# One operand in PSUM for rotary embedding, softmax combination, branch merge and attention division, with an order of steps to match

## The chip, the cores and the metric

The kernel runs on one core of one Trainium2 chip. The metric is the device time of one execution in microseconds (us), taken as the median of several runs; less is better. Engine names in the rows: PE is TensorE (PEld its weight loads), DVE is VectorE, ACT is ScalarE, POOL is GpSimd, SP is the queue that issues most of the DMAs.

## The reference, cut to what matters

The reference is a two-layer generator trunk with 256 latent and 256 context tokens of width 1024. Each layer normalizes and modulates its input, projects it, and runs three branches: latent attention with a rotary key (A), a long convolution (B) and differential attention (C). Then the branches are merged by sigmoid gates and projected, and an MLP follows. The pieces that the change touches:

```python
def apply_rope(x, cos, sin):                      # rotary embedding
    x1, x2 = x[..., :half], x[..., half:]
    return concatenate([x1 * cos - x2 * sin, x2 * cos + x1 * sin], axis=-1)
...
p = softmax(q @ k.T * scale); o = p @ v           # attention; the division comes after p @ v here
...
o = o1 - lam * o2                                 # differential attention: two maps, then a norm
rmsnorm(o, g) * (1.0 - lam_init)
...
m = g_a * (ya @ w_br_a) + g_b * (yb @ w_br_b) + g_c * (yc @ w_br_c)    # merge
y = m @ w_out
```

Layer 0 works on all 512 tokens, layer 1 on the 256 latent ones only (its keys and values still take 512).

## The kernel before, in words

**Matmuls.** Every large product is made of three matmuls: each operand is split into a high part (a cast, `hi`) and the rest (a subtraction, `lo`), and hi·hi, hi·lo and lo·hi are summed in one PSUM bank (`mm3`, L278 to L280). So for each piece of weights (a "unit" of 128x1024) somebody must cast (L230) and somebody subtract (L218), and each activation goes through the same in `split2` (ACT copies, L284, DVE subtracts, L285).

**PSUM.** There are eight banks of 128x512: two each named `s`, `g` and `t`, one `o`, one `mod`. `bank(tag)` hands out the banks of a tag in turn, and the next user of a bank waits until its last reader is done. `bank2` lets some steps of layer 1 take `mod` instead. SBUF scratch comes from a ring of nine 128x512 tiles (`t2k`).

**Steps.** The program is a list of 562 steps, built by `layer`; `ORDER`, a permutation written into the file, says in which order they are emitted. Within that, the framework places the instructions of neighbouring steps among each other on each engine. `CHOICE` is a table that says for a key which engine does a piece of work (`A` ACT, `D` DVE, `P` POOL, `m` the `mod` bank); what isn't in it goes to a default engine. Keys: `hi`/`lo` + number are a unit's cast and subtraction, `rb` + number the second product of a rotary embedding, `kh` a head's key cast, `v` a value copy, `dup` a duplicate row of the differential attention's operands, `tr` the copy of transposed maps, `sq`, `xe`, `mh`, `ml`, `r`, `rl`, `yx` single elementwise operations.

**The pieces that change.** `rope` works in place on a product in PSUM: a shuffle that swaps halves into SBUF (L794), the product with the cosines into SBUF (L795), the product of the shuffled copy with the sines, on DVE or POOL by `CHOICE` (L797), and the sum back to PSUM (L798). It is called 26 times, 13 in each layer. In the differential attention, step `A` computes two maps (matmul L1221, row maximum L807, Exp on ACT L156, the latter into SBUF tiles), a small factor (L1233, L1234) and the combination of both maps (L1238); step `B` transposes the result on PE (L834), step `C` multiplies it with the values, step `N` normalizes. `normalized` (L818 on) divides by the softmax sums, which PE has transposed into a bank `t` (L827, L828). `branch` multiplies three products with three gates (L1332) and adds them up (L1336).

Of the kernel before, what the change touches and what calls it, by code (L numbers as in the profile page):

```python
# [9 lines left out]
F32 = mybir.dt.float32  # L10
F32R = mybir.dt.float32r
AF = mybir.ActivationFunctionType
ALU = mybir.AluOpType
# [110 lines left out]
def backbone_kernel(ctx: ExitStack, tc: tile.TileContext, t, out):  # L124
# [394 lines left out]
    def startup(first_weights):  # L519
        with tc.tile_pool(name="filt", bufs=1, side="right") as fp, tc.tile_pool(name="start", bufs=1) as sp:  # L520
# [234 lines left out]
            SP.dma_start(out=rs, in_=t["rope_sin"])  # L755
# [34 lines left out]
    def rope(ps, rows, scr=True):  # L790

        a, b = t2k(), t2k()
        v = ps[rows, 0:NL]
        DVE.stream_shuffle(out=b[rows, 0:NL], in_=v, mask=SWAP16)  # L794
        DVE.tensor_tensor(out=a[rows, 0:NL], in0=v, in1=rc[rows, :], op=ALU.mult)  # L795
        rope.n = getattr(rope, "n", -1) + 1
        ENG[pick(f"rb{rope.n}", "D")].tensor_tensor(out=b[rows, 0:NL], in0=b[rows, 0:NL], in1=rs[rows, :], op=ALU.mult)  # L797
        DVE.tensor_tensor(out=v, in0=a[rows, 0:NL], in1=b[rows, 0:NL], op=ALU.add)  # L798
# [18 lines left out]
    def normalized(o, sums, nt, key):  # L817

        s, r, rb = t2k(), smp.tile([128, 4, 2], F32, tag="sr", name="sr", bufs=2), t2k()
        nb = nt // 128  # L820
        cp("oe" + key)(s[:, :nt], o[:, :nt])
        DVE.reciprocal(out=r[:, :nb], in_=sums[:, :nb])
        cp("rb" + key)(rb[:, :nt].rearrange("p (j i d) -> p j i d", i=2, d=64),
                       r[:, :nb].unsqueeze(3).to_broadcast([128, nb, 2, 64]))
        pt = bank("t")
        for j in range(nb):
            PE.transpose(pt[:, j * 128:(j + 1) * 128], rb[:, j * 128:(j + 1) * 128], ident)  # L827
        DVE.tensor_tensor(out=s[:, :nt], in0=s[:, :nt], in1=pt[:, :nt], op=ALU.mult)  # L828
        return s
# [327 lines left out]
    def diff(l, nt):  # L1157
# [49 lines left out]
        def A(h, u):  # L1207
            def f():
# [7 lines left out]
                for mi in range(2):  # L1216
# [11 lines left out]
                    p = t2k()  # L1228
# [32 lines left out]
        def N(p):  # L1261
            def f():
                ps = bank("t")
                S["last"] = PE.matmul(ps[:, :nt], lhsT=blk64, rhs=box["sq", p][:, :nt], start=True, stop=True).ins
                r = rstd_of(ps[:, :nt], 64, nt)
                s = t2k()
# [22 lines left out]
    def merge(l, nt, early):  # L1289
# [31 lines left out]
        def branch(n):  # L1321
            def f(u):
                acc = None
                for b, (y, k0, nk, tag) in enumerate((("ya", 0, 4, "s"), ("yb", 4, 2, "s"), ("yc", 6, 2, "g"))):
# [7 lines left out]
                    DVE.tensor_tensor(out=g[:, :nt], in0=g[:, :nt], in1=ps[:, :nt], op=ALU.mult)  # L1332
                    if acc is None:
                        acc = g
                    else:
                        DVE.tensor_tensor(out=acc[:, :nt], in0=acc[:, :nt], in1=g[:, :nt], op=ALU.add)  # L1336
# [341 lines left out]
```

## Time and profile before

| | before |
|---|---|
| median of 3 runs | 1338.29 us (1335.92 to 1344.03) |
| profiled execution, its own time | 1338.25 us |
| its span in the profile | 1336.5 us |
| granted TensorE clock, mean | 0.986 of full speed |
| PE busy | 1286.9 us, 96% |
| DVE busy | 868.0 us, 65% |
| ACT busy | 587.7 us, 44% |
| POOL busy | 278.9 us, 21% |

How to read it: the busy time of an engine is the sum of its instructions' durations without overlaps. PE has 49.6 us of the span in which it does nothing; where it works at a granted clock below 1.00, its instructions take longer. A table of stretches (busy time of each engine and granted clock in each) shows where both lie, and the list of waits says for which instruction of which engine PE waited.

### The profile page before, as it was taken

The page shows a single profiled execution, that of the slowest core. Times are in us where ns is not written, and L with a number is a line of the kernel's source. Part 1 is how long each engine was busy: PE and PEld are TensorE (multiplying, and loading weights), DVE is VectorE, ACT ScalarE, POOL GpSimd, SP SyncE. Part 2 cuts the span into 40 slices and gives each one's busy share as a digit, 9 for nine tenths or more (in the row PEclk, how much of TensorE's full clock was granted, in tenths as well). Part 3 has the DMA queues.
Part 4 walks back from the last instruction along what each step waited for, and adds up shares of the span by engine and source line. Part 5 has one row for each costly group of instructions (what it writes and reads, how often), then busy time and mean ns, then how long its engine had stood idle before and what let it go on. Part 6 is the DMA issues. An engine that isn't in the chain of part 4 may idle for free.

```text
span 1336.5 us, 19918 instructions
## 1 busy us (share of the span) xinstructions
PE 1286.9 (96%) x7934; PEld 1080.9 (81%) x7934; DVE 868.0 (65%) x1406; ACT 587.7 (44%) x1034; POOL 278.9 (21%) x247
## 2 busy tenths in 40 slices
PE   5999999999999999999999999998998999999997
PEld 3566776578888898787787877996887999999997
DVE  4776636955243568886585774587667568876565
ACT  4455543664222334432332332364646655645343
POOL 3212031310002102220100112022234344240210
PEclk8899999999999999999999999998999999999999
DMA  9643243443233324655554553332132455455652
GB/s 278 168 165 106 69 136 99 146 158 95 86 103 95 115 76 141 208 186 174 171 191 141 165 163 119 98 115 68 49 109 79 127 175 176 158 181 181 192 187 95
DMA packets 159791, 185.21 MB, mean 139 GB/s; under 512 B 4880, under 2 KB 149233, under 8 KB 157650
## 3 DMA queue, kind: packets, MB, share of 16 engines
q1 hardware_dynamic: 158162, 182.27, 43.5%
q0 software_dynamic: 928, 1.54, 0.4%
q8 instruction: 62, 1.02, 0.3%
q14 instruction: 31, 0.25, 0.1%
q10 hardware_dynamic: 608, 0.14, 0.0%
HBM read 182.88 MB, written 1.05 MB: 138 GB/s over the span
## 4 chain that ended last, share of the span: by engine, by line
PE 71%; DVE 8%; ACT 2%; DMA 2%; issue 1%; POOL 0%; DVEq 0%; ACTq 0%; SPq 0%; POOLq 0%
PE g L278 13%; PE g L279 13%; PE g L280 13%; PE s L278 8%; PE s L280 8%; PE s L279 8%; DMA raw<-in_w_fc_dram 1%; PE o L847 1%; PE t L834 1%; DVE d L1176 1%; DVE hlo L488 1%; DVE wlo L218 1%; ACT whi L230 1%; DVE t L485 1%; PE mod L346 1%
## 5 line engine op out<-in xcount | busy, mean ns | idle before, releaser
L230 ACT CAST whi<-raw 128x1024 fp32r<-128x1024 f32 x203 | 212.7, 1050 | 442.9 <-PE g L279 206.7
L278 PE MATMUL g<-hhi,whi 128*128 128x512 f32 (+2 forms) x1040 | 355.0, 342 | 5.6 <-ACT ge L1305 1.6
L280 PE MATMUL g<-hhi,wlo 128*128 128x512 f32 (+2 forms) x1040 | 353.0, 340 | 0.5 <-DVE wlo L218 0.5
L279 PE MATMUL g<-hlo,whi 128*128 128x512 f32 (+2 forms) x1040 | 353.0, 340 | 0.2 <-DVE hlo L505 0.2
L218 POOL TENSOR_TENSOR wlo<-raw,whi 128x512 fp32r<-128x512 f32 x144 | 201.9, 1422 | 637.6 <-ACT whi L230 517.2
L218 DVE TENSOR_TENSOR wlo<-raw,whi 128x1024 fp32r<-128x1024 f32 x158 | 197.1, 1249 | 154.1 <-ACT whi L230 147.0
L278 PEld LDWEIGHTS g<-hhi,whi 128*128 128x128 f32 x1040 | 196.1, 189 | 37.5 <-issue 7.0
L279 PEld LDWEIGHTS g<-hlo,whi 128*128 128x128 f32 x1040 | 196.8, 189 | 23.5 <-issue 0.8
L280 PEld LDWEIGHTS g<-hhi,wlo 128*128 128x128 f32 x1040 | 196.9, 189 | 23.2 <-DVE wlo L218 0.9
L382 DVE SCALAR_TENSOR_TENSOR macc<-modr,spad,macc 128x1024 f32<-128x1024 f32 x84 | 111.4, 1356 | 13.0 <-DMA modr<-in_w_mod_dram 12.2
L1358 DVE SCALAR_TENSOR_TENSOR x<-s,modT,x 128x256 f32<-128x256 f32 x95 | 43.4, 479 | 74.5 <-PE s L280 74.3
L280 PE MATMUL s<-hid0h,wlo 128*128 128x512 f32 (+1 forms) x256 | 87.0, 340 | 0.0
L279 PE MATMUL s<-hid0l,whi 128*128 128x512 f32 (+1 forms) x256 | 86.7, 339 | 0.0
L278 PE MATMUL s<-hid0h,whi 128*128 128x512 f32 (+1 forms) x256 | 86.6, 338 | 0.0
L280 PE MATMUL s<-hid1h,wlo 128*128 128x256 f32 (+1 forms) x224 | 72.7, 325 | 0.0
L278 PE MATMUL s<-hid1h,whi 128*128 128x256 f32 (+1 forms) x224 | 72.6, 324 | 0.0
L279 PE MATMUL s<-hid1l,whi 128*128 128x256 f32 (+1 forms) x224 | 72.2, 323 | 0.0
L156 ACT ACTIVATE t<-s,sm 128x512 f32<-128x512 f32 (+1 forms) x91 | 55.4, 612 | 36.9 <-DVE sm L807 36.2
L807 DVE TENSOR_REDUCE sm<-s 128x1 f32<-128x512 f32 (+1 forms) x75 | 51.3, 687 | 25.3 <-PE s L280 20.0
L278 PEld LDWEIGHTS s<-hid0h,whi 128*128 128x128 f32 x256 | 48.4, 189 | 7.3 <-ACT whi L230 0.8
L279 PEld LDWEIGHTS s<-hid0l,whi 128*128 128x128 f32 x256 | 48.0, 187 | 5.9
L280 PEld LDWEIGHTS s<-hid0h,wlo 128*128 128x128 f32 x256 | 48.1, 188 | 5.7
(465 smaller groups left out, 2411.1 us busy)
## 6 DMA issues: line engine op xcount, KB each, us to landing
raw<-in_w_fc_dram SPq DMA_DIRECT2D x64, 1024.0 KB, 5.4
raw<-in_w_in_dram SPq DMA_DIRECT2D x34, 1024.0 KB, 5.3
modr<-in_w_mod_dram SPq DMA_DIRECT2D x48, 512.0 KB, 4.1
raw<-in_w_mod_dram SPq DMA_DIRECT2D x16, 1024.0 KB, 5.0
mq<-in_w_mod_dram SPq DMA_DIRECT2D x16, 512.0 KB, 7.5
raw<-in_w_out_dram SPq DMA_DIRECT2D x8, 1024.0 KB, 5.3
raw<-in_w_in_dram SPq DMA_DIRECT2D x8, 512.0 KB, 3.9
raw<-in_w_br_a_dram SPq DMA_DIRECT2D x8, 512.0 KB, 3.6
```

Of the source, the lines that this page charges most:

```text
L156: ins = ACT.activation(out=out, in_=in_, func=func, **kw).ins
L218: e.tensor_tensor(out=u.lo[:, a:a + w], in0=src[:, a:a + w], in1=u.hi[:, a:a + w].bitcast(F32), op=ALU.subtract)
L230: cp(f"hi{u.id}")(u.hi, src)
L278: PE.matmul(ps, lhsT=ah, rhs=bh, start=first and i == 0, stop=False)
L279: PE.matmul(ps, lhsT=ah, rhs=bl, start=False, stop=False)
L280: PE.matmul(ps, lhsT=al, rhs=bh, start=False, stop=last and i == n - 1)
L346: PE.matmul(box["ps"][32 * j:32 * j + 32, :], lhsT=spad[:, kt, :], rhs=raw[:, 512 * j:512 * (j + 1)], start=kt == 0, stop=kt == KT - 1)
L382: DVE.scalar_tensor_tensor(out=a, in0=raw, scalar=sv, in1=a, op0=ALU.mult, op1=ALU.add)
L485: DVE.scalar_tensor_tensor(out=tt, in0=x[:, kt, c], scalar=amul[l][:, w, kt, s:s + 1], in1=r, op0=ALU.mult, op1=ALU.mult)
L488: DVE.scalar_tensor_tensor(out=hb["lo"][:, kt, c], in0=tt, scalar=sh, in1=hb["hi"][:, kt, c].bitcast(F32), op0=ALU.add, op1=ALU.subtract)
L807: DVE.tensor_reduce(out=sm[:, c0:c0 + nseg], in_=ps.rearrange("p (s k) -> p s k", s=nseg), axis=AX.X, op=ALU.max, negate=True)
L1358: DVE.scalar_tensor_tensor(out=x[:, n, c], in0=ps[:, c], scalar=modT[l][:, goff + n, s:s + 1], in1=x[:, n, c], op0=ALU.mult, op1=ALU.add)
```

## The change

`rope` now multiplies the product in PSUM by the sines first, into SBUF, then by the cosines in place, shuffles the sine product within SBUF, and adds it to PSUM; all four are on DVE, and the keys `rb` are gone. The table of sines is shuffled once at the start so that the result is the same: it is loaded to a new tile `rst`, and a shuffle writes `rs`. `normalized` writes its result to the PSUM bank of the sums when branch A calls it. In the differential attention the second map stays in its PSUM bank (Exp writes in place), and the combination reads it from there; in step `N` the reciprocal root and the scaled result are written to the PSUM bank of the sum of squares. In `branch` the second and third gated products are written back to the PSUM banks of the products, and the last sum is written there too, from where `split2` reads it. `ORDER` has some 25 steps moved by one to three places, and two moved further in layer 1 (step 425, an inverse transform of the convolution branch, and step 450, the normalization of the first pair of heads); the moved steps of the layer 0 MLP are parts of the second layer's modulation, which issue their DMAs from SP. `CHOICE` gains 22 entries and loses 19, 13 of them `rb`.

```diff
-            SP.dma_start(out=rs, in_=t["rope_sin"])
+            rst = fp.tile([128, NL], F32, name="rst")
+            SP.dma_start(out=rst, in_=t["rope_sin"])
+            DVE.stream_shuffle(out=rs, in_=rst, mask=SWAP16)
...
-        DVE.stream_shuffle(out=b[rows, 0:NL], in_=v, mask=SWAP16)
-        DVE.tensor_tensor(out=a[rows, 0:NL], in0=v, in1=rc[rows, :], op=ALU.mult)
-        rope.n = getattr(rope, "n", -1) + 1
-        ENG[pick(f"rb{rope.n}", "D")].tensor_tensor(out=b[rows, 0:NL], in0=b[rows, 0:NL], in1=rs[rows, :], op=ALU.mult)
-        DVE.tensor_tensor(out=v, in0=a[rows, 0:NL], in1=b[rows, 0:NL], op=ALU.add)
+        DVE.tensor_tensor(out=a[rows, 0:NL], in0=v, in1=rs[rows, :], op=ALU.mult)
+        DVE.tensor_tensor(out=v, in0=v, in1=rc[rows, :], op=ALU.mult)
+        DVE.stream_shuffle(out=b[rows, 0:NL], in_=a[rows, 0:NL], mask=SWAP16)
+        DVE.tensor_tensor(out=v, in0=v, in1=b[rows, 0:NL], op=ALU.add)
...
-        DVE.tensor_tensor(out=s[:, :nt], in0=s[:, :nt], in1=pt[:, :nt], op=ALU.mult)
-        return s
+        to = pt if key[0] == "m" else s
+        DVE.tensor_tensor(out=to[:, :nt], in0=s[:, :nt], in1=pt[:, :nt], op=ALU.mult)
+        return to
...
-                    p = t2k()
+                    p = ps if mi else t2k()
...
-                r = rstd_of(ps[:, :nt], 64, nt)
-                s = t2k()
+                r = rstd_of(ps[:, :nt], 64, nt, ps[:, :nt])
+                s = ps
...
-                    DVE.tensor_tensor(out=g[:, :nt], in0=g[:, :nt], in1=ps[:, :nt], op=ALU.mult)
+                    to = g if acc is None else ps
+                    DVE.tensor_tensor(out=to[:, :nt], in0=g[:, :nt], in1=ps[:, :nt], op=ALU.mult)
                     if acc is None:
                         acc = g
                     else:
-                        DVE.tensor_tensor(out=acc[:, :nt], in0=acc[:, :nt], in1=g[:, :nt], op=ALU.add)
+                        to = ps if b == 2 else acc
+                        DVE.tensor_tensor(out=to[:, :nt], in0=acc[:, :nt], in1=ps[:, :nt], op=ALU.add)
+                        acc = to
```

`CHOICE`, the entries that matter near the waits of the rows: new are `hi132`, `hi139`, `lo130`, `lo140`, `lo150`, `v1.3`, `dup1.0.0.1` on DVE and `hi129`, `hi133`, `hi141`, `hi148` on POOL; gone are `kh1.0` from DVE (so ACT does it), `v0.3` from DVE and the `rb` from POOL; two `m` entries (`bktd1.0.0`, `bktm1.3.0`) are gone. `ORDER`, an excerpt of layer 1's differential attention:

```diff
-    (409, 425), (426, 434), 436, (434, 436), 437, 440, 438, 441, 439, (442, 444), 425, (444, 447), 448, 447, 449,
-    453, (450, 453), (454, 461), ...
+    (409, 425), (426, 434), 436, 439, 434, 437, 440, 435, 438, (441, 447), 448, 447, 449,
+    453, (451, 453), 450, 425, (454, 461), ...
```

## Rows read from the trace of the kernel before

**Rows 1.** The page: span, and busy time of each engine.

```profile
span 1336.5 us, 19918 instructions
PE 1286.9 (96%) x7934; PEld 1080.9 (81%) x7934; DVE 868.0 (65%) x1406; ACT 587.7 (44%) x1034; POOL 278.9 (21%) x247
```

**Rows 2.** Forty equal stretches: length, busy time (instructions), granted clock, DMA share, GB/s.

```profile
233.80:267.20 33.40, 30.24 (x163) 19.17 (x162) 30.12 (x58) 21.47 (x54) 12.63 (x13) 1.00 0.41 147
...
367.40:400.80 33.40, 33.40 (x145) 27.01 (x144) 14.36 (x18) 9.52 (x12) 3.25 (x2) 1.00 0.34 105
...
901.80:935.20 33.40, 27.49 (x160) 22.78 (x161) 24.93 (x53) 15.90 (x29) 8.26 (x10) 0.85 0.24 72
...
1002.00:1035.40 33.40, 28.87 (x201) 26.17 (x201) 24.49 (x48) 20.76 (x43) 13.94 (x14) 0.95 0.27 78
```

**Rows 3.** Waits of PE over the span: for whom, us in total, times, longest.

```profile
PE t L834 <- DVE t L1238: 4.8, 5, 1.9
...
PE g L278 <- DVE x L1076: 2.4, 1, 2.4
```

**Rows 4.** DVE in order of time, layer 1: start, duration, what [idle before].

```profile
1006.08 0.45 DVE L794 STREAM_SHUFFLE t<-g 128x256 f32<-128x256 f32 x1
...
1008.62 1.50 DVE L798 TENSOR_TENSOR g<-t 128x256 f32<-128x256 f32 x1 [1.19 <-POOL t L797]
...
1013.19 0.75 DVE L1238 SCALAR_TENSOR_TENSOR t<-t,sm 128x512 f32<-128x512 f32 x1
```

**Rows 5.** POOL in order of time, the same place.

```profile
1007.85 0.74 POOL L797 TENSOR_TENSOR t<-t,rs 128x256 f32<-128x256 f32 x1
1008.54 1.29 POOL L218 TENSOR_TENSOR wlo<-raw,whi 128x512 fp32r<-128x512 f32 x1
```

**Rows 6.** PE in order of time, the same place.

```profile
1013.99 0.66 PE L834 MATMUL t<-ident,t 128*128 128x128 f32 x4 [1.90 <-DVE t L1238]
1015.70 0.38 PE L278 MATMUL g<-hhi,whi 128*128 128x256 f32 x1 [1.05 <-DVE d L1176]
```

**Rows 7.** Two stretches of 4 us there, columns as in rows 2.

```profile
1012.00:1016.00 4.00, 1.05 (x7) 0.72 (x7) 3.74 (x11) 2.91 (x7) 0.95 (x2) 1.00 0.01 2
1016.00:1020.00 4.00, 4.00 (x23) 4.00 (x22) 3.82 (x8) 2.00 (x5) 0.00 (x0) 0.57 0.11 12
```

**Rows 8.** DVE in order of time, layer 0.

```profile
233.89 1.32 DVE L1234 SCALAR_TENSOR_TENSOR sm<-ss,nlam,sm 128x1 f32<-128x1 f32 x1
...
235.74 1.26 DVE L1238 SCALAR_TENSOR_TENSOR t<-t,sm 128x512 f32<-128x512 f32 x1
...
239.30 1.73 DVE L1238 SCALAR_TENSOR_TENSOR t<-t,sm 128x512 f32<-128x512 f32 x1
```

**Rows 9.** PE in order of time, layer 0, the wait behind the last of these.

```profile
241.08 0.33 PE L834 MATMUL t<-ident,t 128*128 128x128 f32 x1 [1.49 <-DVE t L1238]
```

**Rows 10.** Groups by line and shape: busy us, mean ns of one | idle before.

```profile
L458 DVE TENSOR_TENSOR o<-o,t 128x256 f32<-128x256 f32 x26 | 11.1, 427 | 4.2 <-ACT t L454 4.0
...
L1336 DVE TENSOR_TENSOR t<-t 128x512 f32<-128x512 f32 x12 | 8.3, 692 | 0.4
L1332 DVE TENSOR_TENSOR t<-t,s 128x512 f32<-128x512 f32 x12 | 8.2, 684 | 5.7 <-PE s L280 5.7
...
L797 POOL TENSOR_TENSOR t<-t,rs 32x256 f32<-32x256 f32 x9 | 6.8, 759 | 32.2 <-DVE t L794 24.7 <-issue 4.6 <-ACT kh L977 2.9
L797 DVE TENSOR_TENSOR t<-t,rs 32x256 f32<-32x256 f32 x9 | 3.7, 409 | 0.1
```

**Rows 11.** ACT writing to SBUF and to PSUM, by line and shape.

```profile
L454 ACT ACTIVATE t<-x 128x512 f32<-128x512 f32 x2 | 1.3, 631 | 0.5 <-DVE x L1358 0.5
...
L448 ACT ACTIVATE o<-x 128x512 f32<-128x512 f32 x2 | 1.2, 603 | 0.9 <-DVE x L1358 0.8
```

**Rows 12.** DVE in order of time: layer 0's first normalization, from L429 on.

```profile
276.12 0.69 DVE L429 TENSOR_SCALAR t<-t 128x512 f32<-128x512 f32 x1 [2.17 <-PE t L1264]
...
283.39 0.68 DVE L285 TENSOR_TENSOR ycl<-t,ych 128x512 fp32r<-128x512 f32 x1
```

73 rows, old and new, of tables (CHOICE, ORDER) are left out of this document.

## The prediction, as it was put on record

> **What bounds the kernel now.** I read the page's busy times first. PE is busy for 1286.9 of 1336.5 us, DVE for 868.0 [rows 1], so PE sets the time, and a change that touches no matmul can only win back the 49.6 us in which PE does nothing and the stretches in which its granted clock is low. Second, the forty equal stretches: through the layer 0 merge and MLP, from 267 to 868 us, PE misses under 1 us in all, and the stretch 367.40:400.80 stands for those [rows 2]. Whatever the change does there, to the merge of layer 0 and the moved modulation steps, is hidden. Two things are left that it can reach: the layer 0 differential attention (233.80:267.20, PE 30.24 of 33.40, so 3.16 us idle) and two stretches of layer 1 (901.80:935.20, idle 5.91 at a clock of 0.85; 1002.00:1035.40, idle 4.53 at 0.95) [rows 2]. In 15% and 5% of their 33.4 us the low clock costs another 5.0 and 1.7 us at most. That makes 20.3 us, the most that can be won where the change acts; the start and the final norm it hardly touches. Third, the list of waits: the largest one in these places is PE's transposes waiting for the combination of the two maps, 4.8 us in 5 times [rows 3].
>
> **Why those waits are long.** Reader, look at layer 1 around 1007 us. DVE shuffles at 1006.08 [rows 4]; POOL's sine product starts only at 1007.85, and right behind it, at 1008.54, POOL starts a subtraction of 1.29 us [rows 5]. DVE had waited 1.19 us for the product, and its sum (two operands in SBUF) then takes 1.50 us and ends 0.29 us after that POOL subtraction [rows 4, 5], where the same kind of sum with an operand in PSUM takes 0.43 (256 elements, x26) [rows 10]. So a DVE instruction with two SBUF operands waited for POOL's. Everything on DVE behind it is late, up to the combination at 1013.19 [rows 4], and PE stands still for 1.90 us and then 1.05 us [rows 6]. After that its clock falls: 0.57 in 1016 to 1020, following 1.05 us of work in the 4 us before [rows 7]. In layer 0 two combinations take 1.26 and 1.73 us [rows 8] instead of the 0.75 of the one in layer 1 [rows 4], and PE waits 1.49 us behind the second [rows 9].
>
> **Rotary embedding.** Before, 4 operations, in 13 of the 26 calls 3 on DVE and one on POOL; after, 4 on DVE. The costs: product from PSUM 0.41 [rows 10] (the DVE form of L797, which differs only in its source), product in place in PSUM 0.43 (L458) [rows 10], shuffle 0.45 [rows 4], sum 0.43. The shuffle now reads SBUF, which the trace doesn't show; between 0.41 (a product) and 0.45 (the shuffle from PSUM) I take 0.45. DVE gains 13 x 0.41 = 5.3 us of work, POOL loses 13 x 0.76 = 9.9 us [rows 10]. On PE's path this lies at one place for certain, the call of rows 4: DVE's idle 1.19 and the excess of 1.50 over 0.43, 1.07, go; one more product of 0.41 comes: 1.19 + 1.07 - 0.41 = **1.85 us off**, of 2.95 us of PE's waits there. I count it whole, since ACT's and DVE's steps between the sum and the combination all follow that sum. What remains of PE's wait is 1.1 us; a wait of 1.49 us in layer 0 [rows 9] lies in a stretch whose clock stays at 1.00 [rows 2], so I expect no fall here: 4.00 x 0.43 = **1.7 us off** [rows 7], bounds 0 and 1.7.
>
> **Combination from PSUM.** It loses its waits for POOL: in layer 0, 1.26 and 1.73 become 0.75 each, 0.51 + 0.98 = **1.5 us off**; bounds 0 (the small factor before it, L1234, keeps two SBUF operands and took 1.32 us [rows 8], so the wait may only move) and 2.9, what PE waits there in all. The price of a PSUM operand by itself is nothing: the sum of two SBUF tiles takes 692 ns, the product with one in PSUM 684 [rows 10]. Exp in place writes PSUM: ACT takes 603 ns to PSUM and 631 to SBUF for the same square [rows 11], so nothing to pay either.
>
> [...]
>
> **Banks held longer.** This is the change's real cost, a wait that it adds. The second map's bank is now free only after the combination, not after Exp. There are two `s` banks, and layer 0 has no other for the maps: the matmul of a step's second map (L1221) must wait for the combination of the step before, and PE takes its instructions in order, so gates and projections queued behind it wait too, and the transposes behind those. Until now PE waited 4.8/5 = 0.96 us at a combination [rows 3], of a step further back. Layer 0 has 12 such steps, so 11 transitions: between 0 and 11 x 0.96 = 10.6 us. I take **1 us on**, near the lower end, because matmuls of gates and projections can be placed ahead of it, and only the stretch where DVE is nearly full, 30.12 of 33.40 us [rows 2], is at risk: one wait of 0.96. In layer 1 some maps go to `mod`, which adds slack. Normalization: bank `t` is held from L429, 276.12, to the end of the split, 284.07, 8 us instead of 0.7 [rows 12], four times, and the transposes use `t` as well; 0 to 4 us (one wait of 0.96 each), I take **0.5 us on**. The divided values of branch A hold `t` over a cast and a subtraction, 0.63 [rows 11] + 0.68 [rows 12] = 1.3 us more, eight times; no wait of PE's list [rows 3] names a reader of that bank, so 0, and 1 us on at most if one does. Merge: the third product's bank waits for sum, cast and subtraction. In layer 0 the cover is a saturated PE [rows 2], with a gate of 24 matmuls before the bank's next turn; in layer 1 0 to 1 us; I take 0.
>
> **Order, engines, start.** `kh1.0` to ACT takes a cast of 512 elements (nearest row a subtraction of 0.68 us [rows 12]) off DVE just before the conv step that PE waits 2.4 us for [rows 3]; ACT then does it behind its own work: **0.5 us off**, bounds 2.4 off and 1.2 on (`lo140`, a whole subtraction, comes to DVE in the same stretch). The other choices move casts and subtractions that are a unit ahead, and the moved steps change places with neighbours: 0, bounds 2 either way. SP's and POOL's queues carry the same loads; the modulation loads that moved lie where PE has no wait. The new shuffle of the sine table at the start waits for its DMA, with DVE's preparation of layer 0's inputs queued behind it: 0, as the table isn't used before layer 0's rotary keys, and 1 us on if it lands late.
>
> **Sum.** -1.85 - 1.7 - 1.5 - 0.5 + 1 + 0.5 = -4.05 us. The profiled execution took 1338.25 us (span 1336.5 and 1.75 around it), as good as the median 1338.29. So **1334.2 us**.
>
> **Rivals.** First, the other side, slower: the second map's bank becomes PE's wait. All other terms stay (-4.05 - 1 = -5.05), the 11 transitions cost 10.6: 1338.25 + 5.55 = 1343.8 us. It decides from about six waits of 0.96 on. For it: DVE is nearly full there, and the combination comes last in a step. Against: a combination now takes 0.75, and L1221 never appears among PE's waits today. Chance 0.2. Second, nothing comes of it: DVE's next two-SBUF instruction, the factor L1234, takes over the wait for POOL (its 1.32 is the sign [rows 8]), and 5.3 us more work on DVE eats the rest: 1338, chance 0.15. Third, the fitted order wins more than I can trace: both layer 1 stretches lose most of idle and low clock, say 13 of their 17.1 us, and layer 0 its 1.5: 1324, chance 0.1. It would need the 2.4 us wait for the conv step [rows 3] to vanish, which only `kh1.0` and the casts address. The forecast has 0.55, from 1329 to 1338.
>
> [...]
>
> **Range and chances.** From the third rival's side to somewhat beyond the first's, with 0.1 left out on either side: 1322 to 1347. Runs lie 8 us apart, so 1% (13.4 us) is about what can be told from no change. Faster by over 1%, below 1324.9, is half of the third rival and a tail of the forecast: 0.11. Slower by over 1%, above 1351.7, is the first rival with waits twice as long: 0.05. Within 1%: 0.84.
>
> **What would show it.** Right: the sums of the rotary embedding and the combinations never exceed 0.5 and 0.8 us beside POOL work; PE's wait near 1014 is about 1 us and the clock behind it stays at 1.00; POOL's busy time falls; no wait of PE at L1221. Wrong: L1221 or transposes among PE's longest waits, with a DVE combination or the normalization's split as releaser; L1234 still over 1 us where POOL subtracts; a new fall of the clock in either attention.

## The result, and the profile after

The changed kernel takes 1327.46 us (median of 5 runs, 1325.55 to 1328.16), the kernel before 1337.83 us (median of 5). The ratio is 0.9929, with a 95% interval of 0.9912 to 0.9946: 0.7% faster, some 9.5 us. The forecast was 1334.2, 4.05 us off: the direction held, and the forecast had less than half of the size. The time lies inside the stated range (1322 to 1347), but below the 1329 to 1338 that the forecast itself was given. The profiled execution took 1327.46 us as well (span 1325.7); lines of the changed kernel are numbered one to six later than before (L1238 is now L1241).

The page, as in [rows 1]:

```profile
span 1325.7 us, 19880 instructions
...
PE 1281.5 (97%) x7934; PEld 1077.5 (81%) x7934; DVE 868.3 (66%) x1426; ACT 579.7 (44%) x1027; POOL 262.9 (20%) x233
```

PE's idle time fell only from 49.6 to 44.2 us, and its busy time by 5.4, though the matmuls are the same 7934: half of the gain lies in matmuls that ran at a higher clock (its mean went from 0.986 to 0.989) or overlapped better. POOL has 16 us less, DVE the same sum as before. The stretches of [rows 2]:

```profile
233.80:267.20 33.40, 32.06 (x190) 21.31 (x191) 28.43 (x61) 23.27 (x58) 8.10 (x9) 1.00 0.47 169
...
901.80:935.20 33.40, 27.86 (x170) 22.68 (x169) 26.46 (x55) 14.17 (x29) 5.65 (x7) 0.90 0.25 77
1002.00:1035.40 33.40, 32.32 (x247) 29.13 (x246) 26.87 (x52) 25.13 (x54) 13.60 (x13) 1.00 0.42 127
```

PE's idle time in them was 3.16, 5.91 and 4.53 us and is 1.34, 5.54 and 1.08; the clocks were 1.00, 0.85 and 0.95. The third stretch is nearly repaired, the first more than halved, the second is not. Part of the first has only moved, since the same work now stands at other times: from 201 to 267 us together, PE's idle time fell from 4.7 to 3.3 us. The list of PE's waits, as in [rows 3], says the same: no transpose waits for a combination any more, and the conv step's 2.4 us is still there (2.5). The last line is new.

```profile
PE g L279 <- DVE x L1079: 2.6, 2, 2.5
...
PE g L279 <- DVE t L1079: 2.2, 2, 1.2
...
PE s L1224 <- ACT t L157: 1.4, 2, 1.1
```

The place of [rows 4 to 7] again, first DVE and then POOL in order of time, then two stretches of 4 us of that attention:

```profile
1000.77 0.42 DVE L797 TENSOR_TENSOR t<-g,rs 128x256 f32<-128x256 f32 x1
1001.11 0.42 DVE L798 TENSOR_TENSOR g<-g,rc 128x256 f32<-128x256 f32 x1
...
1001.45 0.45 DVE L799 STREAM_SHUFFLE t<-t 128x256 f32<-128x256 f32 x1
...
1002.38 0.42 DVE L800 TENSOR_TENSOR g<-g,t 128x256 f32<-128x256 f32 x1
...
1005.86 0.75 DVE L1241 SCALAR_TENSOR_TENSOR t<-s,sm,t 128x512 f32<-128x512 f32 x1
```

```profile
1001.80 2.54 POOL L219 TENSOR_TENSOR wlo<-raw,whi 128x512 fp32r<-128x512 f32 x2
```

```profile
1012.00:1016.00 4.00, 3.81 (x28) 3.29 (x29) 3.87 (x6) 3.04 (x7) 2.24 (x2) 1.00 0.90 266
1016.00:1020.00 4.00, 4.00 (x32) 3.76 (x31) 3.83 (x8) 3.24 (x6) 0.61 (x1) 1.00 0.84 251
```

See the sum L800: it runs at 1002.38, in the middle of POOL's two subtractions (1001.80 to 1004.34), and takes 0.42 us; before, a sum beside one such subtraction took 1.50 [rows 4, 5]. No fall of the clock follows. Over the whole kernel the groups by line and shape show the same, before:

```profile
L1238 DVE SCALAR_TENSOR_TENSOR t<-t,sm 128x512 f32<-128x512 f32 x16 | 13.4, 839 | 0.3
...
L1234 DVE SCALAR_TENSOR_TENSOR sm<-ss,nlam,sm 128x1 f32<-128x1 f32 x16 | 7.6, 476 | 0.2
...
L798 DVE TENSOR_TENSOR g<-t 128x256 f32<-128x256 f32 x8 | 5.5, 691 | 1.9 <-POOL t L797 1.8
```

and after:

```profile
L1241 DVE SCALAR_TENSOR_TENSOR t<-s,sm,t 128x512 f32<-128x512 f32 x16 | 12.0, 749 | 0.4
...
L1237 DVE SCALAR_TENSOR_TENSOR sm<-ss,nlam,sm 128x1 f32<-128x1 f32 x16 | 4.5, 280 | 0.5
...
L800 DVE TENSOR_TENSOR g<-g,t 128x256 f32<-128x256 f32 x8 | 3.4, 429 | 0.1
```

### The profile page after: what moved, and what is told of

Read it like the earlier page. It is cut to its first block, busy times and chain, and to the rows that moved or that the text cites. A ratio compares the mean times of both kernels' runs of the same rounds, so it can differ in the third digit from the quotient of the medians.

```text
span 1325.7 us, 19880 instructions
## 1 busy us (share of the span) xinstructions
PE 1281.5 (97%) x7934; PEld 1077.5 (81%) x7934; DVE 868.3 (66%) x1426; ACT 579.7 (44%) x1027; POOL 262.9 (20%) x233
## 3 DMA queue, kind: packets, MB, share of 16 engines
HBM read 182.88 MB, written 1.05 MB: 139 GB/s over the span
## 5 line engine op out<-in xcount | busy, mean ns | idle before, releaser
L231 ACT CAST whi<-raw 128x1024 fp32r<-128x1024 f32 x197 | 206.7, 1051 | 429.8 <-PE g L280 201.5
L279 PE MATMUL g<-hhi,whi 128*128 128x512 f32 (+2 forms) x1040 | 354.3, 341 | 4.3 <-DVE d L1179 1.7
L219 POOL TENSOR_TENSOR wlo<-raw,whi 128x512 fp32r<-128x512 f32 x138 | 187.6, 1380 | 647.3 <-ACT whi L231 508.2
L279 PEld LDWEIGHTS g<-hhi,whi 128*128 128x128 f32 x1040 | 195.4, 188 | 36.2 <-issue 4.7
L279 PE MATMUL s<-hid0h,whi 128*128 128x512 f32 (+1 forms) x256 | 86.7, 339 | 0.0
L279 PE MATMUL s<-hid1h,whi 128*128 128x256 f32 (+1 forms) x224 | 72.8, 325 | 0.0
L279 PEld LDWEIGHTS s<-hid0h,whi 128*128 128x128 f32 x256 | 48.4, 189 | 8.2 <-issue 1.7
L157 ACT ACTIVATE t<-s,sm 128x512 f32<-128x512 f32 (+1 forms) x67 | 40.8, 614 | 26.0 <-DVE sm L809 25.7
```

The lines of the kernel that those rows point to most:

```text
L157: ins = ACT.activation(out=out, in_=in_, func=func, **kw).ins
L219: e.tensor_tensor(out=u.lo[:, a:a + w], in0=src[:, a:a + w], in1=u.hi[:, a:a + w].bitcast(F32), op=ALU.subtract)
L231: cp(f"hi{u.id}")(u.hi, src)
L279: PE.matmul(ps, lhsT=ah, rhs=bh, start=first and i == 0, stop=False)
```

## The experiments

**Theories.** The prediction's: the operands win by themselves, through the stalls beside POOL, and `ORDER` and `CHOICE` are worth next to nothing (0.5 us, for `kh1.0`). Its rivals: the fitted order and choices carry the gain; or the two only pay together, since a table of choices is fitted to one set of operations. The kernels take the change apart along these lines. Where an experiment keeps the old rotary embedding it also keeps the old `rb` entries, so that it is the old one in full.

**How segments are read.** The table sums up all profiles: for each kernel, how many us it gained (-) or lost (+) against the kernel before in five segments. They end at the cast of the first query head of layer 0 (101.5 us in the kernel before), at the last matmul of the squares of layer 1's queries (888.6), at the last forward-transform matmul of the convolution (1000.5), at the last matmul of the normalization `N` (1062.5) and at the end of the span. Each entry is the difference of two leads, from one execution per kernel. Kernels that share what lies in a segment agree there within about 0.8 us (the operands with layer 0's choices against the operands alone: +3.9 and +4.3, then -5.6 and -5.5). The start is the exception: it differs by up to 6 us between these profiles, one execution each does not tell why, and nothing below rests on it. A profile can also stand some us off its kernel's median: by 5.5 us in experiment 1 (where the start has +4.3) and by 2.7 us in experiment 8 (where the start has nothing).

| kernel | start | layer 0 | layer 1, to 1000 | layer 1, 1000 to 1062 | rest | span |
|---|---|---|---|---|---|---|
| changed kernel | +0.2 | -4.5 | -0.5 | -6.9 | +0.9 | -10.8 |
| operands, old order and choices | +4.3 | +0.5 | +4.3 | -5.5 | +0.1 | +3.7 |
| order and choices, old operands | -1.8 | -1.7 | +2.9 | -1.1 | +2.4 | +0.7 |
| rotary alone | -1.3 | -3.2 | +3.4 | -3.5 | -0.2 | -4.8 |
| map alone | +0.7 | +1.0 | -1.6 | -4.2 | +1.2 | -2.9 |
| rest of the operands alone | -0.2 | +2.9 | -0.5 | 0.0 | -0.6 | +1.6 |
| operands, new order, old choices | -1.0 | +0.6 | +2.8 | -6.7 | -0.5 | -4.8 |
| operands, old order, new choices | -1.6 | -4.6 | -1.5 | -5.4 | +0.1 | -13.0 |
| changed kernel, old rotary | 0.0 | +1.8 | +2.8 | -4.7 | -0.1 | -0.2 |
| new choices alone | +1.7 | -2.5 | +0.2 | 0.0 | -0.4 | -1.0 |
| operands, choices of layer 0 | +1.0 | -3.8 | +3.9 | -5.6 | +0.2 | -4.3 |
| operands, choices of layer 1 | +0.4 | 0.0 | -2.2 | -5.4 | -0.2 | -7.4 |
| as the eighth, without the map | +2.9 | -3.6 | -1.4 | -4.8 | +0.2 | -6.7 |

**1. All operands, old order and choices.** The kernel before with the edits of `rope`, `normalized`, the second map, step `N` and `branch`, and nothing of `ORDER` or `CHOICE` (the `rb` entries have no reader any more).

> All operand edits, with the order and the engine choices of before. Theory A (the operands win: DVE no longer waits for POOL): 4 to 8 us faster than before, PE's wait behind the combination near 1014 us at 1 us or less and no fall of the clock behind it. Theory B (the new order and choices win, the operands alone bring nothing because banks are held longer): within 2 us of before, or slower, with new waits of PE behind the second map's bank (L1224 there) or the transposes.

Measured: 1336.45 us against 1337.04, ratio 0.9995 (0.9980 to 1.0011). The operands alone win nothing that can be measured, though they win 5.5 us between 1000 and 1062. They lose 4.3 just ahead of that, in layer 1's first attention. DVE and POOL there in order of time:

```profile
913.62 1.37 DVE L218 TENSOR_TENSOR wlo<-raw,whi 128x1024 fp32r<-128x1024 f32 x1
915.02 0.48 DVE L1076 SCALAR_TENSOR_TENSOR t<-g,vec,t 128x255 f32<-128x255 f32 x1
...
916.06 1.19 DVE L1081 TENSOR_TENSOR t<-u,t 128x256 f32<-128x256 f32 x1
```

```profile
915.68 1.28 POOL L218 TENSOR_TENSOR wlo<-raw,whi 128x512 fp32r<-128x512 f32 x1 [1.77 <-ACT whi L230]
```

The weights' subtraction on DVE now stands ahead of the convolution's steps (before, it started at 909.46, after them), and the sum L1081, with both operands in SBUF, takes 1.19 us instead of 0.42: it ends at 917.25, 0.29 us after POOL's subtraction. It is the stall of [rows 4, 5] in a new place, in an operation that the change does not touch. The three other kernels with the new rotary embedding and layer 1's old choices (experiments 3, 5 and 10) show it as well, at 1.17 to 1.18 us, and lose 2.8 to 3.9 us in that segment; in every other kernel this sum takes 0.41 to 0.43 us. PE has two waits here:

```profile
916.17 0.47 PE L278 MATMUL g<-wvh,cnh 128*128 128x512 f32 x1 [1.58 <-DVE t L1078]
...
918.28 0.80 PE L278 MATMUL g<-wvh,cnh 128*128 128x512 f32 x1 [1.18 <-DVE vtok L951]
```

The first is for the step L1078 behind the weights' subtraction, and not for the stall, which begins only after that step. The second waits for DVE's copy `vtok`, which stands behind the slow sum; of its 1.18 us the 0.77 that the sum lost are the stall's share, by estimate. The kernel before had two waits at this place too, 1.03 us for ACT and 1.14 for `vtok`, beside a fast sum. The segment between the table's marks, first in the kernel before and then here, and the stretch here in which the clock falls:

```profile
888.60:1000.50 111.90, 104.32 (x755) 90.82 (x753) 76.67 (x157) 60.21 (x123) 30.54 (x34) 0.95 0.28 79
...
893.40:1009.60 116.20, 105.78 (x754) 91.73 (x754) 80.04 (x164) 61.05 (x125) 26.00 (x28) 0.94 0.27 76
918.00:924.00 6.00, 5.71 (x17) 4.84 (x18) 0.62 (x2) 2.64 (x4) 1.43 (x2) 0.50 0.28 97
```

PE's idle time is 7.6 us before and 10.4 here; of the 2.8 us more, 1.5 are waits for the casts of the queries (`qh`, 2.8 us in place of 1.3). What the clock costs (length times what it lacks of 1.00, an estimate from these rows; in the kernel before a 128x256 matmul of L279 took 0.28 us at 1003.73, at a clock of 1.00, and 0.41 at 1017.05, in the stretch at 0.57 [rows 7]) is 5.6 and 7.0 us; the kernel before has a stretch at 0.50 as well, from 924 to 930. So the stall is a link of the loss, but its own 0.77 us is the smaller part of the 4.3.

**2. New order and choices, old operands.**

```diff
 # the changed kernel, with the operands of before put back, and:
+    "rb1": "P", "rb4": "P", "rb5": "P", ... (13 entries)
```

> The new order and engine choices with the old operands, the sine products on DVE and POOL as before. Theory A: within 2 us of before, and PE still waits 1.5 us or more in layer 1 behind a combination that follows a blocked sum of a rotary embedding. Theory B: 7 us or more faster than before, near the changed kernel.

Measured: 1339.01 against 1337.04, ratio 1.0015 (1.0001 to 1.0029). Without the operands the fitted order and choices are 2 us slower. PE still waits 2.2 us for a combination in layer 1, as the theory of the operands expected. So neither half wins by itself, and both theories that name one of them fell. The 2.9 us that this kernel loses in layer 1's first attention come without the slow sum of experiment 1 (0.42 us here); their cause stays open.

**3. The rotary embedding alone**, with the shuffled table of sines:

```diff
-        DVE.stream_shuffle(out=b[rows, 0:NL], in_=v, mask=SWAP16)
...
+        DVE.tensor_tensor(out=v, in0=v, in1=b[rows, 0:NL], op=ALU.add)
```

> Only the rotary embedding is changed, the rest as before. Theory A: 2 to 4 us faster, all of it at one place in layer 1 (about 1006 to 1020 us), where DVE's idle time for POOL's product and the 1.50 us sum are gone. Theory B: within 1 us.

Measured: 1334.26 against 1337.04, ratio 0.9981 (0.9969 to 0.9993). It wins 3.2 us in layer 0 and 3.5 from 1000 to 1062, and loses 3.4 in layer 1's first attention: three places, where one was expected.

**4. The second map alone:**

```diff
-                    p = t2k()
+                    p = ps if mi else t2k()
```

> Only the second map stays in PSUM. Theory A: 0 to 1.5 us faster, the combinations at 0.75 us where POOL subtracts. Theory B: slower by 1 us or more, up to 10, with PE waiting at the second map's matmul for the combination of the step before.

Measured: 1334.23 against 1337.04, ratio 0.9985 (0.9970 to 1.0001). The interval just includes 1. Theory B's wait, of the second map's matmul for a combination, shows once, for 0.4 us. Now compare the stretch of [rows 2] at 1002 us in this kernel and in the one of experiment 3:

```profile
1002.00:1035.40 33.40, 31.51 (x230) 28.34 (x231) 27.08 (x56) 23.43 (x50) 15.80 (x16) 1.00 0.33 100
```

```profile
1002.00:1035.40 33.40, 30.67 (x225) 27.65 (x224) 26.26 (x57) 24.17 (x52) 15.80 (x15) 1.00 0.31 95
```

Either edit alone removes the fall of the clock (0.95 to 1.00) and much of the 4.53 us of idle time (2.6 and 1.8 us): -4.2 and -3.5 us in that segment, and both together -5.5. They repair one chain, so their gains do not add. The map does it without touching the slow sum. POOL and DVE in this kernel:

```profile
1006.26 0.74 POOL L797 TENSOR_TENSOR t<-t,rs 128x256 f32<-128x256 f32 x1 [7.20 <-DVE t L794]
...
1007.03 1.50 DVE L798 TENSOR_TENSOR g<-t 128x256 f32<-128x256 f32 x1
```

The sum takes 1.50 us as before, but DVE's idle 1.19 us ahead of it are gone: POOL now computes the sine product ahead of both its subtractions, where before one of them (1006.59) came first. So what the map won at this place came with a new order on POOL; its own operand in PSUM saved nothing here, since the combination takes 0.75 us either way.

**5. New operands and new order, choices of before.**

```diff
 # the changed kernel, but CHOICE as in the kernel before
```

> The changed kernel with the engine choices of before (the rotary products all on DVE): the order of steps alone goes with the operands. Theory C (the order is what keeps the operands' gain, by what it puts ahead of the conv steps and the maps of layer 1): 7 us or more faster than before. Theory D (the engine choices keep it, by relieving DVE and ACT around 900 to 930 us): 1 to 3 us faster than before.

Measured: 1335.93 against 1337.73, ratio 0.9990 (0.9975 to 1.0005). With the old choices the gain is gone.

**6. New operands and new choices, order of before.**

```diff
 # the changed kernel, but ORDER as in the kernel before
```

> The changed kernel with the order of before: the engine choices alone go with the operands. Theory C: 1 to 3 us faster than before, with PE waits of 3 us or more in layer 1's first attention (902 to 969 us). Theory D: 7 us or more faster.

Measured: 1325.26 against 1337.73, ratio 0.9903 (0.9885 to 0.9921), the fastest kernel of all. The new order wins nothing: without it the kernel is 2.2 us faster, with intervals that just overlap, and the table shows why: the order wins 1.5 us from 1000 to 1062 and gives back 1.0 ahead of it and 0.8 behind it. The first attention of layer 1, between the marks that experiment 1 shows:

```profile
882.40:992.80 110.40, 102.37 (x749) 88.57 (x748) 81.77 (x169) 56.15 (x120) 25.17 (x27) 0.97 0.28 80
```

By the same estimate the clock costs 3.3 us here and 7.0 in experiment 1; PE's idle time is 8.0 and 10.4. In place of 1.58 and 1.18 us PE waits 1.20 and 0.18. The sum L1081 is fast again, and POOL has no subtraction of weights beside it until 911.49, only two casts (898.56 and 907.67) and the convolution's own sums L1084 (900.76 and 904.51). DVE in order of time:

```profile
902.10 1.22 DVE L218 TENSOR_TENSOR wlo<-raw,whi 128x1024 fp32r<-128x1024 f32 x1
...
904.02 0.42 DVE L1081 TENSOR_TENSOR t<-u,t 128x256 f32<-128x256 f32 x1
```

**7. The rest of the operands alone** (division, step `N`, merge).

```diff
+        to = pt if key[0] == "m" else s
...
+                r = rstd_of(ps[:, :nt], 64, nt, ps[:, :nt])
+                s = ps
...
+                        to = ps if b == 2 else acc
```

> Only the divided values, the normalization and the merge are changed, in the order of before. If the parts add up, these cost what the rotary embedding (2.5 off) and the second map (2 off) won and all operands together (0.6 off) did not: 3 to 4 us slower than before, with waits of PE behind a bank t or g that is held longer. If they do not add up, because each edit shifts where instructions are placed in the same stretch of layer 1: within 1.5 us of before.

Measured: 1338.96 against 1337.73, ratio 1.0000 (0.9986 to 1.0014; the two medians alone would give 1.0009): nothing that can be measured, the second of the two expectations. One of PE's waits shows a price, though: in layer 0's merge PE now stands still for 0.8 us for `ml`, the subtraction that follows the last sum, and it did not do so there before (from 313 to 468 us it was busy for 155.00 of 155 us and is for 154.18).

**8. The changed kernel with the old rotary embedding.**

```diff
-        DVE.tensor_tensor(out=a[rows, 0:NL], in0=v, in1=rs[rows, :], op=ALU.mult)
...
+        ENG[pick(f"rb{rope.n}", "D")].tensor_tensor(out=b[rows, 0:NL], in0=b[rows, 0:NL], in1=rs[rows, :], op=ALU.mult)
```

> The changed kernel with the old rotary embedding, its sine products on DVE and POOL as before. If the rotary edit is worth in the new order what it won in layer 0 and in layer 1's second attention (3 us each by the stretches of its run alone): 4 to 7 us slower than the changed kernel, so 3 to 6 us faster than before. If it is worth only its 2.5 us alone: 7 us faster than before.

Measured: 1335.47 against 1337.73, ratio 0.9981 (0.9965 to 0.9998), where the changed kernel has 0.9929. Within the change some 7 us (0.0052 of 1337.8) hang on the rotary embedding, which won 2.5 by itself in experiment 3. The table puts them into layer 0 (+1.8 in place of -4.5), the first attention of layer 1 (+2.8, -0.5) and the stretch from 1000 (-4.7, -6.9). That is 11.8 us, too much, as the profiled execution was 2.7 us slower than its kernel's median; only the places are to be read from it. The first attention loses its 2.8 us without the slow sum of experiment 1 (0.42 us here), and why stays open.

**9. The new choices alone**: old operands, old order.

```diff
+    "hi22": "D", "lo2": "D", "v1.3": "D", "lo130": "D", "hi129": "P", "hi133": "P", ... (22 entries)
-    "kh1.0": "D", "lo60": "D", "sq20": "D", "v0.3": "D", "bktd1.0.0": "m", "bktm1.3.0": "m",
```

> The kernel before with the newly fitted table of choices alone (old order, old operands; the copy of the sums that the old merge needs is kept). Old order with new choices and the changed operands was 12.5 us faster than before, the operands alone 0.6. Theory 'the choices win by themselves': 6 to 9 us faster, near 1330, because their gains stand in stretches that hold few changed operands (layer 0's attention, the normalization, the head of layer 1). Theory 'choices and operands win only together': within 2 us of before, since new order and choices with old operands were 2 us slower. In the second case the stretch of layer 1's differential attention, 1000 to 1062 us, stays as long as before within 1 us.

Measured: 1335.42 against 1337.65, ratio 0.9988 (0.9973 to 1.0003). That is 1.6 us by the ratio, the case of a gain only together. They win 2.5 us in layer 0, and nothing in layer 1. The stretch at 1002 us is as bad as before, with a lower clock in place of some of the idle time:

```profile
1002.00:1035.40 33.40, 30.44 (x202) 27.27 (x201) 24.83 (x51) 19.87 (x43) 12.67 (x13) 0.90 0.27 78
```

**10 and 11. The operands with half of the new choices each**, in the old order: those of the start and layer 0, and those of layer 1.

```diff
 # layer 0: dup0.0.1.2, hi22, lo2, lo60, ml0.0.0.3, r0.0.2, sq20, trd0.2.2, v0.3, xe0.1 to xe0.3, yx0.0
 # layer 1: bktd1.0.0, bktm1.3.0, dup1.0.0.1, hi129, hi132, hi133, hi139, hi141, hi148, kh1.0, lo130, lo140, lo150, trm1.1.1, v1.3
```

> Changed operands, old order, and of the new choices only those of steps of the start and of layer 0. Theory 'each choice pays in its own stretch': 4 to 5 us faster than the changed operands with old order and choices (1336.5), so near 1332: 3 in layer 0's attention (up to 313 us) and 1.6 round the normalization (485 us), with layer 1 from 888 us on as slow as it was with the old choices. Theory 'the gain is one repaired place in layer 1': within 1 us of 1336.5.

> Changed operands, old order, and of the new choices only those of steps of layer 1. Theory 'each choice pays in its own stretch': 4 to 6 us faster than the changed operands with old order and choices (1336.5), so near 1331.5: 1.5 at the head of layer 1 and 3 to 4 in its first attention, from 896 to 963 us, where the moved load of weights ahead of the convolution's steps had cost the rotary change its gain. Theory 'the gain is one repaired place in layer 1': 10 to 12 us faster, near 1325. Layer 0 as with the old choices.

Measured: 1332.72 and 1331.09 against 1337.65, ratios 0.9960 (0.9946 to 0.9975) and 0.9955 (0.9937 to 0.9973). Each half pays in its own layer and nowhere else: layer 0's give -3.8 in layer 0 in place of +0.5 and leave layer 1's first attention at +3.9; layer 1's leave layer 0 at 0.0 and turn that +4.3 into -2.2. Beyond the operands alone (0.9995) they are worth 0.0035 and 0.0040, together 0.0075, where all choices at once gave 0.0092 (experiment 6); the intervals cover the difference. It is not one repaired place.

**12. The fastest kernel without the map**: experiment 6 with the second map copied to SBUF again.

```diff
-                    p = ps if mi else t2k()
+                    p = t2k()
```

> The fastest so far (changed operands, old order, new choices, 1325.3) with the combination of maps put back to its copy of the second map in SBUF. Theory 'the map is worth what it is worth alone': 3 us slower (alone it won 3.1 over both layers), near 1328. Theory 'its worth is the stretch of layer 1's differential attention as well': 5 to 6 us slower, near 1331, half of the 5.5 us that this stretch lost with the operands being the map's. Theory 'rotary alone carries it': within 1 us.

Measured: 1328.98 against 1337.65, ratio 0.9934 (0.9917 to 0.9951). The map is worth 0.9934 - 0.9903 = 0.0031, about 4 us with intervals that overlap, and so not to be told from the 2.0 us that it won alone. It is not needed for the stretch from 1000 to 1062, which keeps -4.8 of its -5.4 us without it.

## Why the prediction was right in direction and too small

**Rotary embedding and clock, -1.85 and -1.7, together -3.55 us: right in mechanism and place.** The idle wait for POOL and the sum's 1.50 us are gone, PE's wait of 1.90 [rows 6] with them, and the clock stays at 1.00. In size, rotary alone won 3.5 us in that segment (PE's idle time went from 5.16 to 3.34 us, the clock from 0.97 to 1.00); with the map 5.5, in the whole change 6.9. Over the whole kernel the edit alone also won 3.2 us in layer 0 and lost 3.4 in layer 1's first attention. The forecast had neither, so it is luck that its 2.5 us in all lie near the term. I had expected a wait of about 1 us to stay at the combination, and none did: the one that is left is 0.81 us for another operand. The four operations cost what their rows said (420 to 450 ns). Both sides of the stall were measured: L800 with one SBUF operand takes 0.42 us in the middle of POOL's work, L1081 with two takes 1.19 (experiment 1).

**Combination, -1.5 us in layer 0: right in the waits, not shown in the time.** Its durations fell to the undisturbed 0.75, PE's 4.8 us behind it went, and layer 0 from 201 to 267 us lost 1.4 us of idle time in the whole change. But the map alone took the stalls off the combinations as well (mean 748 ns), and layer 0 got 1.0 us slower by it, which is little more than the table's uncertainty. Its 2.0 us (experiment 4) came from layer 1, where I had credited it with nothing, by the order on POOL. The second rival, that L1234 takes over the wait, fell: its mean went from 476 to 280 ns, though one of the 16 still takes 0.89 us (236.86) and one of the four over 128x2 takes 0.69 (286.57). The operand in PSUM cost the combination nothing: 749 ns, where the undisturbed one from SBUF took 0.75 us [rows 4].

**Banks.** For the second map I put 1 us on, of up to 10.6. The wait came at the line that I had named (L1221, now L1224), 1.4 us in layer 0, against the sign that no wait would stand there. But it waits for the Exp of a first map, which frees an `s` bank, and not for the combination; the forecast wait for a combination shows only in experiments 1 and 4, 0.4 us in each. PE and ACT there:

```profile
234.24 0.50 PE L1224 MATMUL s<-d,d 96*128 96x512 f32 x1 [1.12 <-ACT t L157]
```

```profile
233.41 0.69 ACT L157 ACTIVATE t<-s,sm 128x512 f32<-128x512 f32 x1
```

The matmul L279 at 234.57 stood behind this wait, though its weights had been cast by 228.43: here PE did take its instructions in order, as the term supposed. The first rival, this wait eleven times over, fell. Division, `N` and merge, +0.5 in sum, measured 0 to within 1.9 us (experiment 7); the merge's 0 was 0.8 us too good, since a place in the saturated stretch had no cover.

**`kh1.0`, -0.5 us of a 2.4 us wait: wrong.** The wait is 2.5 us now. I took DVE's cast for the last link before the conv step. It was ACT. The kernel before, ACT in order of time and then DVE:

```profile
918.27 0.56 ACT L1071 ACTIVATE x<-g,vec 128x256 f32<-128x256 f32 x1
```

```profile
918.13 0.68 DVE L977 CAST kh<-g 64x512 fp32r<-64x512 f32 x1 [0.99 <-PE g L280]
918.87 0.48 DVE L1074 SCALAR_TENSOR_TENSOR x<-g,vec,x 128x255 f32<-128x255 f32 x1
```

DVE's step needs ACT's x, which ended at 918.83; the cast ran beside it, ended at 918.81 and cost nothing. In the changed kernel DVE has nothing else to do and stands still for 1.94 us for that same ACT step, which comes right after a cast of weights of 1.05 us (912.32, the step at 913.27).

**The step that failed: "the other choices ...: 0, bounds 2 either way".** With the old operands this holds nearly (1.6 us, experiment 9). With the new ones the choices are worth 12 us (0.9995 to 0.9903): 5 in layer 0 and 6 in layer 1's first attention. I had costed the table as an addition to the operands, and looked for it only at the waits of the kernel before. But the edits shift DVE's work, and with the old table the convolution's step behind a subtraction of weights then comes later (PE waits 1.58 us for it, 1.20 with the new table) and the stall beside POOL comes up at another operation with two SBUF operands (L1081, experiment 1). That much is shown; how the 6 us split is not: the stall itself is 0.77 us, more of it is clock, and experiments 2 and 8 lose 2.9 and 2.8 us there without the stall. The third rival was near in its number, 1324, and wrong in its cause: it put the gain on the order, which won nothing, and wanted the 2.4 us wait to vanish, which stayed. For the order itself, 0 was right within the intervals.

Of the cause of layer 0's 4.5 us only the split is shown: the choices alone 2.5 (among them PE's waits from 502 to 889 us, 2.14 of idle time before and 0.55 in experiment 9), the rotary embedding alone 3.2, against 2.9 lost by the rest of the operands and 1.0 by the map, and what comes when they meet. Which entry does it stays open; single entries were not tried.

## What to carry to other kernels

Here a stall between two engines belonged to a place in the schedule, not to an instruction: the sum L798 lost its 1.50 us, and the sum L1081, which the change does not touch, then took 1.19. Where one operand goes to PSUM, look on to where the next DVE instruction that works within SBUF alone meets POOL's work, and to what is pushed ahead of what. A table of engine choices that was fitted to one set of operations is part of the change: cost the new operations with the old table and with the new one; here the operations alone won nothing that could be measured, and the choices alone some 1.6 us, by an interval that includes nothing at all. The gains of two edits that shortened the same chain did not add (-4.2 and -3.5 us alone, -5.5 in all operands together), so sum over chains and not over edits.

## What the runs showed of the hardware that was not expected

In the kernel before and in experiments 1, 3, 5 and 10 a DVE sum with two SBUF operands ended 0.28 to 0.29 us after POOL's subtraction: 1010.12 after 1009.83 [rows 4, 5], 917.25 after 916.96 (experiment 1, another operation). A DVE sum that reads one operand from PSUM ran in the middle of the same POOL work in 0.42 us (L800 at 1002.38), where the eight of its shape take 429 ns on average.

Two SBUF operands are not needed for it. In experiment 1 a DVE cast with a single operand, within SBUF, took 1.27 us beside two POOL subtractions (989.83 to 992.36), where the same shape takes 0.28 at 1004.47 in the changed kernel, with POOL idle:

```profile
991.24 1.27 DVE L1181 CAST d<-d 32x256 fp32r<-32x256 f32 x1
```

In the first attention of layer 1 idle time and low clock go together only loosely, by one execution of each kernel: between the table's marks PE was idle for 8.0 us in experiment 6 and the clock cost 3.3 us; in the kernel before it was idle for 7.6 us and the clock cost 5.6.
